# Moving group C's input projections beside group B's attention, and storing the latents of group A unsplit: a two-layer hybrid encoder on one core

## The chip, the cores and the metric

The kernel runs on one core of one Trainium2 chip. The metric is device time in microseconds of one execution of the whole program. All times below come from the profiled execution of the kernel before, or from its three timed runs.

## The reference, cut to what matters

The program computes two encoder layers over 1,024 tokens of width 1,024. A layer has four groups of attention heads side by side, one output projection, and a squared-ReLU MLP.

```
for l in range(DEPTH):                       # DEPTH = 2
    h = rms_norm(x, norm1_g[l])
    proj = h @ w_in[l]
    (a_cq, a_ckv, a_kr, b_q, b_k, b_v, c_q, c_k, c_v, d_q, d_k, d_v) = split(proj)
    y_a = mla_mixer(a_cq, a_ckv, a_kr, ...)  # A: q = rms_norm(cq) @ w_uq, k = rms_norm(ckv) @ w_uk, v = ... @ w_uv
    y_b = diff_mixer(b_q, b_k, b_v, ...)     # B: two softmaxes, p0 - lam * p1
    y_c = swa_mixer(c_q, c_k, c_v, ...)      # C: keys within +-128 tokens, with sinks
    y_d = na_mixer(d_q, d_k, d_v, ...)       # D: neighbourhood on a grid 64 wide
    mix = concat(rms_norm(y_a), y_b, rms_norm(y_c), rms_norm(y_d))
    x = x + mix @ w_out[l]
    h = rms_norm(x, norm2_g[l])
    x = x + square(relu(h @ w_up[l])) @ w_down[l]
return rms_norm(x, final_norm_g)
```

`cq` has 192 columns (128 and 64) and `ckv` has 128. These three pieces, of 128, 64 and 128 rows once transposed, are called the latents here. Every entry is float32.

## The kernel before, in words

**Numbers in two parts.** Everything is held transposed, features on partitions and tokens along the row. A matmul operand is split in two, `hi` (rounded) and `lo` (the rest), and a product takes three matmuls: w_hi x_hi, w_hi x_lo, w_lo x_hi (`passes`, lines 220 to 222). `split` (lines 190 to 199) makes the two parts: one activation on ACT (line 194, or 197 where a gain is multiplied in), and one subtraction, on DVE or POOL through the helper at line 188, or on DVE at line 198 where there is a gain.

**The stages of a layer.** The normed input `xs` is split once into 16 tiles of 128x1024, which fill the pool `big` (16 buffers) completely. Then come these stages:

- The six projections of group B run in two waves.
- Group B's attention (`attn_b`) runs with other projections between its steps. `weave` takes one step of the main work, then as many steps of the fill as the ratio allows. A step of a projection is one half: 24 matmuls of 128x512 into one PSUM tile, and its evacuation.
- Group D's attention (`attn_d`, banded: scores at line 977, transposes at 986, products at 998 and 999), with a fill of its own.
- Group C's attention, then group A's, with the first half of the output projection as fill, and then the rest of the output projection.
- The MLP, which is more than half of the time.

**What is fill for what.** Beside B stand `proj_latent` (three projections, which also make the rotary key of A) and `proj_d` (six projections). Beside D stand `proj_c` (four projections: two of queries, one of keys, one of values) and `latent_up`. `latent_up` loads the latents from DRAM, multiplies them by the up-projections (loaded as `w_lat`) into A's q, k and v, and stores those.

```
fill = chain(self.proj_latent(l, one, xs, rb, tabs, lat, krd, rows), proj_d())
self.weave(chain.from_iterable(self.attn_b(l, t, qb, kb, vb, y["b"]) for t in range(2)),
           fill, self.RB, self.LB, every=self.EV[0])
...
fill = chain(proj_c(), self.latent_up(l, lat, rows, qa, ka, va))
self.weave(self.attn_d(l, qd, kd, vd, y["d"]), fill, self.RD, self.LD, every=self.EV[1])
```

The ratios are `RB = (7, 8)`, eight steps of fill for seven of B, and `RD = (3, 2)`.

**The latents' way.** `latent_parts` squares each half of a latent for the norm (ACT, line 652; PE, line 655), splits it with its gain, and stores both parts to DRAM. `latent_up` loads them as `latp` tiles. The 64-row latent is loaded twice, into the upper and the lower half of a tile. The six `latp` tiles, and `rq` and `rkv` (the norms' rows, spread over all partitions), come from the pool `big`, so each waits until one of the 16 `xs` tiles is free, which is when the last projection that reads it is done.

**What orders the work.** The order of the steps above gives each instruction a priority. A scheduler, when the program is built, then sets one fixed order for each engine, moving ahead what it expects to be ready. An engine executes its list in order: an instruction that waits holds up all that stand behind it. Nearly all DMAs are issued from SP's queue, and one that waits there holds up the others too.

**Other lines the change touches.** `rstd_cols` (line 261) gets column sums by matmuls, and `spread` loads the rows that `rows_of` stored into all partitions. With two groups (`g=2`, only in `sub_norm` of group B) the stored rows of the groups alternate.

Of the kernel before, what the change touches and what calls it, by code (L numbers as in the profile page):

```python
# [13 lines left out]
F = mybir.dt.float32  # L14
R = mybir.dt.float32r
# [5 lines left out]
P = 128  # L21
S = 1024
# [6 lines left out]
T_CQ, T_CQR, T_CKV = 0, 1, 2  # L29
# [69 lines left out]
def layout(i):  # L99

    def padded(a, axis):

        z = np.zeros([1 if n == axis else s for n, s in enumerate(a.shape)], a.dtype)
        return np.concatenate([a, z], axis)

    n = LAYERS
    out = host_constants()
    out["x"] = i["x"][0].T.reshape(8, P, S)
    out["w_in"] = tiles_of(padded(i["w_in"], 2)[:, :, np.concatenate(input_tiles())], 4)

    wo = i["w_out"].reshape(n, 8, P, DM)[:, [2, 3, 6, 7, 4, 5, 0, 1]].reshape(n, DM, DM)
    out["w_out"] = tiles_of(wo, 4)
    out["w_up"] = tiles_of(i["w_up"], 4)
    out["w_down"] = tiles_of(i["w_down"], 4)

    uq = i["mla_w_uq"].reshape(n, 192, 4, 96)
    cols = [uq[..., 64:96].reshape(n, 192, 4, 2, 16).transpose(0, 1, 3, 2, 4).reshape(n, 192, P)]
    cols += [uq[:, :, 2 * t:2 * t + 2, 0:64].reshape(n, 192, P) for t in range(2)]
    q = np.stack(cols, 1)

    q = np.concatenate([q, q[:, :, 128:192]], 2).reshape(n, 6, P, P)
    kv = [i[w][:, None, :, t * P:(t + 1) * P] for w in ("mla_w_uk", "mla_w_uv") for t in range(2)]
    w = np.concatenate([q] + kv + [np.zeros((n, 2, P, P), uq.dtype)], 1)
    out["w_lat"] = w.reshape(n, 3, 4, P, P).transpose(0, 1, 3, 2, 4)
    rpb = padded(i["na_rpb"].reshape(n, 4, 465), 2)
    rpb[..., 465] = NEG
    out["bias"] = rpb[..., neighbours()]
    col = lambda a: a.reshape(n, -1, P).transpose(2, 0, 1).reshape(P, -1)
    gq = np.concatenate([i["mla_q_norm_g"], np.zeros((n, 64), np.float32)], 1)
    sub = np.concatenate([i["diff_subln_g"]] * 2, 1)  # L130
    lam = np.stack([i["diff_lambda_" + s] for s in ("q1", "q2", "k1", "k2")], 1)
    wide = lambda a: np.broadcast_to(a.reshape(1, -1), (P, a.size))
    out["par"] = np.concatenate(
        [col(i["norm1_g"]), col(i["norm2_g"]), i["final_norm_g"].reshape(8, P).T]
        + [col(i["out_g_" + s]) for s in ("mla", "swa", "na")]
        + [col(i["mla_kv_norm_g"]), col(gq), col(sub), wide(i["swa_sinks"])], 1)
    out["lam"] = wide(lam)
    return {k: np.ascontiguousarray(v) for k, v in out.items()}
# [7 lines left out]
class Trunk:  # L146
# [107 lines left out]
    def rstd_cols(self, sq, count, rhs, tag="mm"):  # L254

        nc = self.nc
        g = rhs.shape[1]
        n = sq.shape[1] // P
        ps = self.bank(tag, [P, n * g])
        for t in range(n):  # L260
            nc.tensor.matmul(ps[:, t * g:(t + 1) * g], sq[:, t * P:(t + 1) * P], rhs, start=True, stop=True)
        ms = self.cp.tile([P, n * g], F, tag="ms", name="ms")
        nc.vector.tensor_scalar(ms, ps, 1.0 / count, EPS, ALU.mult, ALU.add)
        return self.rsqrt_cols(ms)
# [15 lines left out]

    def spread(self, dst, rows, j=0, g=1):

        src = rows.rearrange("(t g) p -> g t p", g=g)[j]
        n = dst.shape[0]
        self.load(dst.rearrange("p (t q) -> p t q", t=8), src.partition_broadcast(n))

    def spread_here(self, dst, col):

# [88 lines left out]
    def attention(self, l):  # L377
        nc, tc, d = self.nc, self.tc, self.d
        rb = self.rb
        sbuf = lambda name, side="left": tc.tile_pool(name=f"{name}{l}", bufs=1, reuse_waits="tile", side=side)  # L380
        w_in = lambda t: d["w_in"][l, t]
        dr = lambda shape, name: self.dram.tile(shape, F, tag=name, bufs=1, name=name)
# [3 lines left out]
        qb, kb, vb = dr([2, 2, 4, 16, 2, S], "qb"), dr([2, 2, 4, 16, 2, S], "kb"), dr([4, P, 8, P], "vb")  # L386
        qd, kd, vd = dr([2, 2, P, S], "qd"), dr([2, 2, P, S], "kd"), dr([4, P, 8, P], "vd")
        qc, kc, vc = dr([2, 2, 2, 32, 2, S], "qc"), dr([2, 2, 32, 2, S], "kc"), dr([2, P, 8, P], "vc")
        lat, krd = dr([2, 3, P, S], "lat"), dr([2, 16, 2, S], "krd")
        qa = dr([2, 2, P, S], "qan"), dr([2, 4, 16, 2, S], "qar")  # L390
        ka, va = dr([2, 2, P, S], "kan"), dr([4, P, 8, P], "va")

# [25 lines left out]
        rows = []  # L418
        y = {"b": [], "d": [], "c": [], "a": []}
        with ExitStack() as stack, ExitStack() as att:  # L420
            self.ap = att.enter_context(sbuf("att"))
            with self.banks(mm=2, tr=2, sb=3, pv=1):
                with sbuf("proj", "right") as self.pp:
                    first = [w_in(t) for t in self.WAVES[0]]
                    saved = d["x"]
                    ahead = self.first
                    if l:
                        saved = self.dram.tile([8, P, S], F, tag="saved", bufs=1, name="saved")
                        for k in range(8):
# [12 lines left out]
                    tabs = self.table("32", rb, nc.vector)  # L442
                    self.eng = nc.vector
                    for t in range(2):
                        for ev, b in zip(evacs_b(t), banks):
                            raw = self.ptile()
                            for n in range(2):
                                sl = slice(n * 512, n * 512 + 512)
                                nc.scalar.activation(raw[:, sl], b[n], AF.Copy)
                                ev(n, raw[:, sl])  # L450
                        if t == 0:
                            banks = wave()
                            self.several([w_in(t) for t in self.WAVES[1]], xs, banks)
                        self.eng = nc.gpsimd

                    fill = chain(self.proj_latent(l, one, xs, rb, tabs, lat, krd, rows), proj_d())
                    self.weave(chain.from_iterable(self.attn_b(l, t, qb, kb, vb, y["b"]) for t in range(2)),
                               fill, self.RB, self.LB, every=self.EV[0])
                    self.tails.append(self.mix_b(mix, y["b"], self.gsub[:, l:l + 1]))
                    fill = chain(proj_c(), self.latent_up(l, lat, rows, qa, ka, va))  # L460
                    self.weave(self.attn_d(l, qd, kd, vd, y["d"]), fill, self.RD, self.LD, every=self.EV[1])
                gout = lambda n: self.gout[n][:, l]
                self.tails.append(self.mix_group(mix, 2, y["d"], gout("na")))
# [72 lines left out]
    EV = (.5, .5, .7, 1)  # L536
    EARLY, RC, RA, LA = 4, (8, 1), (3, 1), 0
    WAVES = [(T_BQ[t], T_BK[t], T_BV[t]) for t in range(2)]
    NP, RB, RD, LB, LD = 6, (7, 8), (3, 2), 40, 50

    def weave(self, main, fill=iter(()), ratio=(1, 0), lead=0, end=True, every=1):

# [101 lines left out]
            self.keep(dst[:, :, n * 4:n * 4 + 4].rearrange("h p k e -> p h (k e)"), b.bitcast(F))  # L644
        return then

    def latent_parts(self, y, g, rows, n, dst, squares):

        nc = self.nc
        sl = slice(n * 512, n * 512 + 512)  # L650
        sq = self.part()
        nc.scalar.activation(sq[:rows], y[:rows], AF.Square)
        ps = self.bank("mm", [P, 4])
        for t in range(4):
            nc.tensor.matmul(ps[:, t:t + 1], sq[:rows, t * P:(t + 1) * P], self.ones[:rows, 0:1],
                             start=True, stop=True)
        nc.vector.tensor_copy(squares[:, n * 4:n * 4 + 4], ps)
        self.emit_parts(y[:rows], [(dst[:, :rows, sl].rearrange("a p s -> p a s"), slice(0, rows))],
                        slice(0, rows), g[:rows])

    def proj_latent(self, l, one, xs, rb, tabs, lat, krd, rows_out):


        nc = self.nc
        squares = [self.col("sq%d" % i, 8) for i in range(3)]
        for i, t, g in ((0, T_CQ, self.gq[:, l, 0:1]), (2, T_CKV, self.gkv[:, l:l + 1])):
            yield from one(t, xs, self.ev_plain(rb, lambda n, y: self.latent_parts(y, g, P, n, lat[:, i], squares[i])))
        c, s = tabs

        def ev(n, ps):  # L670
# [8 lines left out]
            self.emit_parts(y[64:112], [  # L679
                (krd[:, :, h, sl].rearrange("a p s -> p a s"), slice(64 + 32 * h, 80 + 32 * h))  # L680
                for h in range(2)], slice(64, 112))
            self.latent_parts(y, self.gq[:, l, 1:2], 64, n, lat[:, 1], squares[1])

        yield from one(T_CQR, xs, ev)
        q, k = squares[0], squares[2]
# [6 lines left out]
    def latent_up(self, l, lat, rows, qa, ka, va):  # L692
# [2 lines left out]
        self.spread(rq, rows[0])  # L695
        self.spread(rkv, rows[1])
        parts = []
        for i, r in ((0, P), (1, 64), (2, P)):
            p = []
            for j in range(2):  # L700
                t = self.big_tile(R, "latp")
                for at in range(0, P, r):
                    self.load(t.bitcast(F)[at:at + r], lat[j, i, :r])
                p.append(t)
            parts.append(tuple(p))
        tabs = self.table("32", rq, nc.gpsimd)
        (qn, qr), kn = qa, ka

# [782 lines left out]
```

## Time and profile before

| What | us |
|---|---|
| Three timed runs | 2729.50, 2731.64, 2728.26 (median 2729.5) |
| The profiled execution | 2728.97 |
| Its span, first to last instruction | 2727.2 |
| PE busy | 2553.1 (94%) |
| DVE busy | 1994.1 (73%) |
| ACT busy | 1430.9 (52%) |
| POOL busy | 1134.5 (42%) |

The mean granted clock of TensorE is 0.967. Matmuls overlap in a pipeline, so that a matmul of 128x512 is shown as some 390 ns long while the next one starts 0.23 us after it; "PE busy" therefore hides small gaps. Times in the views are microseconds from the first instruction, and the first layer's attention lies between 0 and about 700 us, the second one's between about 1372 and 2050 us.

### The profile page before, as it was taken

Reading aid. Unit: us, or ns where it says so; the run is one execution under the profiler, and the core shown is the slowest. Engines: PE = TensorE matmul, PEld = TensorE weight load, DVE = VectorE, ACT = ScalarE, POOL = GpSimd, SP = SyncE. Lnnn points to the kernel's source line nnn. Section 1 sums busy time; section 2 is a strip of 40 time slices with the busy share of each in tenths; the row PEclk is TensorE's granted clock in tenths of the full one; section 3 lists DMA queues with packets and bytes.
Section 4 is the critical chain, followed back from the end, with each engine's and each line's share of the span. In section 5 each row is a group of like instructions: output and inputs, shape, how many; then the busy total and the mean of one; then the engine's idle time right before and its main releaser. Section 6 shows DMA issues by size and latency. Waiting matters only on the chain.

```text
span 2727.2 us, 37613 instructions
## 1 busy us (share of the span) xinstructions
PE 2553.1 (94%) x12298; PEld 2110.1 (77%) x12298; DVE 1994.1 (73%) x3544; ACT 1430.9 (52%) x2547; POOL 1134.5 (42%) x754
## 2 busy tenths in 40 slices
PE   8989988899989999999999899889998999999997
PEld 6778876787778887888877688767886788878886
DVE  7787767674966669787567778677749666687786
ACT  4667757563534444444436676576635344444444
POOL 2555642111245554445435556331013455545552
PEclk9989999999989999999998899899999999999998
DMA  5534597231234447444244345972221444664431
GB/s 175 166 105 126 154 280 241 83 93 40 65 130 156 151 160 267 156 138 142 98 133 138 95 134 157 300 215 71 76 70 44 154 159 149 223 222 150 131 100 62
DMA packets 190516, 389.20 MB, mean 143 GB/s; under 512 B 23712, under 2 KB 30832, under 8 KB 190320
## 3 DMA queue, kind: packets, MB, share of 16 engines
q1 hardware_dynamic: 176496, 361.62, 43.0%
q10 hardware_dynamic: 13824, 25.17, 2.7%
q8 instruction: 98, 1.61, 0.3%
q14 instruction: 98, 0.80, 0.1%
HBM read 263.29 MB, written 123.41 MB: 142 GB/s over the span
## 4 chain that ended last, share of the span: by engine, by line
PE 70%; DVE 14%; DMA 7%; ACT 4%; issue 3%; SPq 1%; POOL 1%; DVEq 0%; ACTq 0%; POOLq 0%
PE u L220 8%; PE u L222 8%; PE u L221 8%; PE mm L220 5%; PE mm L221 5%; PE mm L222 5%; PE p L220 5%; PE p L221 5%; PE p L222 5%; PE sb L804 3%; PE tr L840 2%; DVE p L806 2%; DVE part L188 2%; PE pv L829 2%; PE pv L828 2%
## 5 line engine op out<-in xcount | busy, mean ns | idle before, releaser
L188 POOL TENSOR_TENSOR wl<-raw,wh 128x512 fp32r<-128x512 f32 x448 | 635.1, 1418 | 705.2 <-ACT wh L194 690.1
L194 ACT ACTIVATE wh<-raw 128x512 fp32r<-128x512 f32 x448 | 281.5, 629 | 579.8 <-PE u L221 315.0
L188 POOL TENSOR_TENSOR wl<-ws,wh 128x512 fp32r<-128x512 f32 (+1 forms) x112 | 148.1, 1325 | 456.9 <-ACT wh L194 426.0
L220 PE MATMUL u<-far,wh 128*128 128x512 f32 x768 | 301.5, 393 | 11.5 <-ACT ev L1237 8.3
L188 DVE TENSOR_TENSOR raw<-raw 128x512 f32<-128x512 f32 x256 | 226.4, 890 | 107.4 <-POOL wl L188 56.9
L222 PE MATMUL u<-far,wl 128*128 128x512 f32 x768 | 300.5, 391 | 1.9 <-POOL wl L188 1.9
L221 PE MATMUL u<-far,wh 128*128 128x512 f32 x768 | 300.3, 391 | 0.0
L188 DVE TENSOR_TENSOR ptl<-tr,pth 128x512 fp32r<-128x512 f32 (+2 forms) x384 | 238.3, 628 | 66.6 <-ACT pth L194 64.9
L809 ACT ACTIVATE p<-p,nm 128x1024 f32<-128x1024 f32 x192 | 220.1, 1147 | 99.8 <-DVE nm L806 98.9
L194 ACT ACTIVATE pth<-tr 128x512 fp32r<-128x512 f32 (+2 forms) x384 | 205.6, 546 | 121.0 <-PE tr L840 64.8
L220 PE MATMUL p<-far,wh 128*128 128x512 f32 x640 | 251.7, 393 | 7.6 <-DVE ev L188 7.6
L222 PE MATMUL p<-far,wl 128*128 128x512 f32 x640 | 250.9, 392 | 1.5 <-POOL wl L188 1.5
L221 PE MATMUL p<-far,wh 128*128 128x512 f32 x640 | 251.0, 392 | 0.0
L804 PE MATMUL sb<-stack 96*128 96x512 f32 x640 | 218.5, 424 | 24.7 <-DVE nm L806 24.0
L188 DVE TENSOR_TENSOR far<-act,far 128x512 fp32r<-128x512 f32 x224 | 208.6, 960 | 14.6 <-ACT far L194 14.6
L188 POOL TENSOR_TENSOR p<-p 128x1024 f32<-128x1024 f32 x64 | 154.3, 2415 | 141.1 <-ACT p L893 125.0
L220 PEld LDWEIGHTS u<-far,wh 128*128 128x128 f32 x768 | 145.4, 189 | 43.6 <-ACT ev L1237 9.2
L222 PEld LDWEIGHTS u<-far,wl 128*128 128x128 f32 x768 | 145.0, 189 | 33.2 <-POOL wl L188 2.7
L220 PE MATMUL mm<-xh,wh 128*128 128x512 f32 x416 | 169.4, 407 | 0.8 <-DVE rows L272 0.2
L806 DVE CUSTOM_DVE_ANT_0 p<-sb,zero,nm 128x512 f32<-128x512 f32 x192 | 142.4, 743 | 36.3 <-PE sb L804 32.8
L221 PEld LDWEIGHTS u<-far,wh 128*128 128x128 f32 x768 | 145.3, 189 | 30.2
L221 PE MATMUL mm<-xl,wh 128*128 128x512 f32 x416 | 166.6, 400 | 0.0
(243 smaller groups left out, 6147.0 us busy)
## 6 DMA issues: line engine op xcount, KB each, us to landing
act<-acts SPq DMA_DIRECT2D x224, 256.0 KB
raw<-in_w_up SPq DMA_DIRECT2D x128, 256.0 KB
acts<-ev SPq DMA_DIRECT2D x128, 256.0 KB
raw<-in_w_down SPq DMA_DIRECT2D x128, 256.0 KB
acts<-ev ACTq DMA_DIRECT2D x96, 256.0 KB
ws<-in_w_in SPq DMA_DIRECT2D x76, 256.0 KB
rz<-drows SPq DMA_DIRECT2D x40, 256.0 KB
stack<-kd SPq DMA_DIRECT2D x32, 256.0 KB
```

The lines of the kernel that those rows point to most:

```text
L188: (eng or self.nc.vector).tensor_tensor(out=out, in0=a, in1=b, op=op)
L194: nc.scalar.activation(hi, src, AF.Copy)
L220: mm(ps, w[0], x[0][:, sl], start=start, stop=False)
L221: mm(ps, w[0], x[1][:, sl], start=False, stop=False)
L222: mm(ps, w[1], x[0][:, sl], start=False, stop=stop)
L804: self.nc.tensor.matmul(ps, q[:, qt * P:(qt + 1) * P], k[:, sl], start=i == 0, stop=i == len(passes) - 1)
L806: self.nc.vector.tensor_tensor_reduce(out=p[:, sl], in0=ps, in1=self.zero[:, 0:1].bitcast(F).broadcast_to([P, 512]), scale=-scale, scalar= ...
L809: self.nc.scalar.activation(p, p, AF.Exp, bias=nm[:, 1:2], scale=-1.0, accum_out=z)
L828: nc.tensor.matmul(out, v[:, kt], h[:, sl], start=kt == 0, stop=False)
L829: nc.tensor.matmul(out, v[:, kt], lo[:, sl], start=False, stop=kt == 7)
L840: nc.tensor.transpose(t[:, k * 256 + i * P:k * 256 + (i + 1) * P], p[:, (j * 2 + k) * P:(j * 2 + k + 1) * P], self.ident)
```

## The change

Four edits, all in the attention part:

- `proj_c` becomes the last part of B's fill, and the ratio `RB` becomes `(2, 3)`, three steps of fill for two of B. The 18 steps of B then take 27 steps of fill: 7 of `proj_latent`, 12 of `proj_d`, 8 of `proj_c`. D's fill is `latent_up` alone.
- The latents are stored unsplit, as one part (`latent`), straight from the tile that the evacuation wrote.
- `latent_up` loads each latent once (the 64-row one into both halves of a tile, as before) and splits it there, with the gain: six splits of 128x512. The gain of the 64-row latent is now laid out for both halves.
- For two groups, the columns in `rstd_cols` are ordered by group, so that `spread` reads one contiguous run of 4 KB for each partition where it read eight runs of 512 bytes.

```diff
-    gq = np.concatenate([i["mla_q_norm_g"], np.zeros((n, 64), np.float32)], 1)
+    gq = np.concatenate([i["mla_q_norm_g"], i["mla_q_norm_g"][:, 128:192]], 1)
...
-            nc.tensor.matmul(ps[:, t * g:(t + 1) * g], sq[:, t * P:(t + 1) * P], rhs, start=True, stop=True)
+            nc.tensor.matmul(ps.rearrange("p (g t) -> p t g", g=g)[:, t], sq[:, t * P:(t + 1) * P], rhs,
+                             start=True, stop=True)
...
-        src = rows.rearrange("(t g) p -> g t p", g=g)[j]
-        n = dst.shape[0]
-        self.load(dst.rearrange("p (t q) -> p t q", t=8), src.partition_broadcast(n))
+        src = rows.rearrange("(g t) p -> g (t p)", g=g)[j]
+        self.load(dst, src.partition_broadcast(dst.shape[0]))
...
-        lat, krd = dr([2, 3, P, S], "lat"), dr([2, 16, 2, S], "krd")
+        lat, krd = dr([3, P, S], "lat"), dr([2, 16, 2, S], "krd")
...
-                    fill = chain(self.proj_latent(l, one, xs, rb, tabs, lat, krd, rows), proj_d())
+                    fill = chain(self.proj_latent(l, one, xs, rb, tabs, lat, krd, rows), proj_d(), proj_c())
...
-                    fill = chain(proj_c(), self.latent_up(l, lat, rows, qa, ka, va))
+                    fill = self.latent_up(l, lat, rows, qa, ka, va)
...
-    NP, RB, RD, LB, LD = 6, (7, 8), (3, 2), 40, 50
+    NP, RB, RD, LB, LD = 6, (2, 3), (3, 2), 40, 50
...
-    def latent_parts(self, y, g, rows, n, dst, squares):
+    def latent(self, y, rows, n, dst, squares):
...
+        self.keep(dst[:rows, n * 512:n * 512 + 512], y[:rows])
         sq = self.part()
         nc.scalar.activation(sq[:rows], y[:rows], AF.Square)
...
-        self.emit_parts(y[:rows], [(dst[:, :rows, sl].rearrange("a p s -> p a s"), slice(0, rows))],
-                        slice(0, rows), g[:rows])
...
-        for i, r in ((0, P), (1, 64), (2, P)):
-            p = []
-            for j in range(2):
-                t = self.big_tile(R, "latp")
-                for at in range(0, P, r):
-                    self.load(t.bitcast(F)[at:at + r], lat[j, i, :r])
-                p.append(t)
-            parts.append(tuple(p))
+        for i, (r, g) in enumerate(((P, self.gq[:, l, 0:1]), (64, self.gq[:, l, 1:2]), (P, self.gkv[:, l:l + 1]))):
+            t = self.big_tile(F, "latent")
+            for at in range(0, P, r):
+                self.load(t[at:at + r], lat[i, :r])
+            h, lo = self.big_tile(R, "lath"), self.big_tile(R, "latl")
+            for sl in self.halves():
+                self.split(h[:, sl], lo[:, sl], t[:, sl], g)
+            parts.append((h, lo))
```

More of the change, by code (lines that the diff above doesn't have):

```diff
@@ L645, in to_values @@
         return then
-    def latent_parts(self, y, g, rows, n, dst, squares):
+    def latent(self, y, rows, n, dst, squares):
         nc = self.nc
-        sl = slice(n * 512, n * 512 + 512)
+        self.keep(dst[:rows, n * 512:n * 512 + 512], y[:rows])
         sq = self.part()
@@ L665, in proj_latent @@
         squares = [self.col("sq%d" % i, 8) for i in range(3)]
-        for i, t, g in ((0, T_CQ, self.gq[:, l, 0:1]), (2, T_CKV, self.gkv[:, l:l + 1])):
-            yield from one(t, xs, self.ev_plain(rb, lambda n, y: self.latent_parts(y, g, P, n, lat[:, i], squares[i])))
+        for i, t in ((0, T_CQ), (2, T_CKV)):
+            yield from one(t, xs, self.ev_plain(rb, lambda n, y: self.latent(y, P, n, lat[i], squares[i])))
         c, s = tabs
@@ L681, in ev @@
                 for h in range(2)], slice(64, 112))
-            self.latent_parts(y, self.gq[:, l, 1:2], 64, n, lat[:, 1], squares[1])
+            self.latent(y, 64, n, lat[1], squares[1])
         yield from one(T_CQR, xs, ev)
```

## The prediction

> **What bounds the kernel now.** I read the page first, then a table by stage (the windows view), then the chain of waits of the stage that stands out, then the waits of TensorE in it. The page says that TensorE (PE) is busy nearly throughout.
>
> ```profile
> span 2727.2 us, 37613 instructions
> PE 2553.1 (94%) x12298; PEld 2110.1 (77%) x12298; DVE 1994.1 (73%) x3544; ACT 1430.9 (52%) x2547; POOL 1134.5 (42%) x754
> ```
>
> The change touches only the attention of each layer, so the share of the whole says little. The table by stage shows the end of group B's attention (300 to 343 us), the last projections (343 to 365), group D (365 to 424) and group C (424 to 470), and below them the second layer's last projections, D and C. The columns are busy microseconds of each engine with its instructions, then the granted clock, the DMA engines' busy share, and GB/s.
>
> ```profile
> core 0: us, PE busy (x) PEld busy (x) DVE busy (x) ACT busy (x) POOL busy (x), PEclk, DMA share, GB/s
> 300.00:343.00 43.00, 42.90 (x236) 36.84 (x236) 32.83 (x79) 30.39 (x53) 35.00 (x22) 1.00 0.59 154
> 343.00:365.00 22.00, 21.77 (x123) 18.53 (x122) 12.20 (x32) 11.83 (x29) 5.85 (x5) 1.00 1.00 296
> 365.00:424.00 59.00, 44.67 (x240) 36.65 (x238) 40.00 (x103) 34.08 (x84) 22.06 (x15) 0.91 0.99 286
> 424.00:470.00 46.00, 38.34 (x204) 29.38 (x204) 37.19 (x104) 35.85 (x97) 12.36 (x8) 0.96 0.75 240
> 1690.00:1712.00 22.00, 21.77 (x124) 18.89 (x123) 13.03 (x39) 14.68 (x38) 10.07 (x7) 1.00 0.98 282
> 1712.00:1770.00 58.00, 46.55 (x243) 39.86 (x242) 38.24 (x99) 32.16 (x80) 23.30 (x15) 0.85 1.00 295
> 1770.00:1820.00 50.00, 41.98 (x219) 33.72 (x219) 37.08 (x107) 34.72 (x90) 12.37 (x8) 0.90 0.85 253
> ```
>
> Up to 343 us PE has no gap and the DMA engines are 59% busy. From 343 to 424 they are full, and from 365 on PE is idle for 14.3 of 59 us at a clock of 0.91. The second layer repeats this. So B is PE's stage and D is the DMA engines' stage. The chain of waits, in order of time (start, length, what), says the same:
>
> ```profile
> 358.15 7.51 DMA rkv<-drows
> 365.69 11.75 DMA latp<-lat
> 399.02 5.40 DMA bias<-in_bias
> 404.43 9.07 DMA stack<-kc
> 413.57 9.20 DMA kan<-both
> ...
> 1713.22 10.30 DMA latp<-lat
> 1723.60 11.52 DMA stack<-kd
> ```
>
> The loads of the latents stand on it in both layers. What PE itself waits for in the first layer's D (total, times, longest):
>
> ```profile
> PE mm L720 <- DMA latp<-lat: 2.7, 2, 2.2
> PE mm L221 <- DMA latp<-lat: 2.4, 1, 2.4
> PE mm L220 <- DMA latp<-lat: 1.3, 1, 1.3
> ```
>
> That is 6.4 us of idle PE in a layer, and it is the part of D that the change can reach most directly.
>
> **The projections of C.** They are 4 tiles of 48 matmuls, 192 in a layer. Their spacing, and that of B's products and transposes, is read from the chain, where one step is the time to the next start:
>
> ```profile
> 352.59 0.44 PE tr L840 x4
> 353.03 0.12 PE pv L828
> 353.95 0.23 PE mm L220
> ```
>
> So 192 x 0.23 = 44 us a layer. It looks as if 44 us of PE moved out of a stage with gaps into one without, which would be a loss. It isn't: in the order of PE's instructions before, only 5 projection matmuls stand behind the last one of B, because the scheduler had already pulled C's projections ahead beside B. After the change none do. On PE the move is worth 5 x 0.23 = 1.2 us, which I count as nothing. The POOL work of C's projections (35.00 of 43 us in B's end) is likewise beside B in both, only spread over more steps; I cost it at nothing, with B's PE work as its cover. If that cover were gone, a step of B would wait for POOL's instructions, of 1.3 to 2.4 us each.
>
> What does move is the place of the latents' products. Before, all of B's matmuls stand ahead of the first product of a latent. After, 56 of them (24 transposes, 32 products) stand behind it, and 26 of the 54 latent products stand ahead of B's last matmul. So the `xs` tiles are free, and rq, rkv, the tables and the latents are loaded, while B still has 24 x 0.11 + 32 x 0.12 = 6.5 us of PE work left. The full stretch of DMA begins that much earlier beside PE's work: worth from 0 to 6.5 us a layer. I take half, 3.3, since loads and stacks of D queue at the same place, and SP's list is in order.
>
> **The bytes.** The latents' loads of both layers are these:
>
> ```profile
> latp<-lat SPq DMA_DIRECT2D x8, 512.0 KB
> ...
> latp<-lat SPq DMA_DIRECT2D x8, 256.0 KB
> ```
>
> A layer loads 4 x 512 + 4 x 256 KB = 3.15 MB; half goes, 1.57 MB. At 286 to 296 GB/s that is 5.4 us of DMA time, in a stretch where DMA ends last, and the latp step of the chain (11.75 and 10.30 us) has room for it. The stores halve as well, but beside B, where the DMA share is 0.59: nothing. They now go straight from the tile that holds the evacuated half; there are three such tiles, and one is held until its store has landed. Six stores a layer; the nearest row, a store of B's keys, took this long:
>
> ```profile
> 63.64 4.37 DMA kb<-both
> ```
>
> Against a projection half of 24 x 0.23 = 5.5 us that is covered; if it isn't, the evacuation behind it waits on DVE and PE for its bank, at most some 4 us a layer. I take 0. The contiguous spread touches two loads of 256 KB per call, two calls a layer, one of them in the full stretch: at most 0.9 us (half of 0.52 MB at 290 GB/s), taken as 0.
>
> **The splits.** Six of 128x512 leave B's projections (two of them with half the partitions, which saves no time) and six come to `latent_up`, each one ACT and one DVE instruction. The same forms before:
>
> ```profile
> L198 DVE SCALAR_TENSOR_TENSOR both<-part,par,both 128x512 fp32r<-128x512 f32 x8 | 8.7, 1092 | 1.2 <-ACT both L197 1.2
> L198 DVE SCALAR_TENSOR_TENSOR opl<-x,par,oph 128x512 fp32r<-128x512 f32 x16 | 11.7, 744 | 2.0 <-ACT oph L197 2.0
> L197 ACT ACTIVATE oph<-x,par 128x512 fp32r<-128x512 f32 x16 | 11.5, 716 | 16.1 <-DVE x L188 16.1
> ```
>
> On ACT 6 x 0.72 = 4.3 us, on DVE between 6 x 0.74 = 4.5 and 6 x 1.09 = 6.6. As work they fit: in D's 59 us DVE is idle for 19 and ACT for 25. As latency the first counts: 0.72 + 1.09 = 1.8 us between the latent's landing and its first product. The other two latents can be split while PE does the first one's products. I count 1.8 us a layer, between 0 and 5.4 (all three). What leaves B is worth 0, as PE's list there is full, and at most 6.6 us, if DVE were what B waits for; the row that could say so is this one, for 60 to 343 us:
>
> ```profile
> PE sb L804 <- DVE nm L806: 10.9, 7, 5.0
> ```
>
> Half of it is a single wait in the norms of the latents, which the change keeps, so I stay at 0.
>
> Why the same form takes 744 or 1092 ns shows nearby. These are two DVE instructions on 8 columns, and the POOL instructions beside the first:
>
> ```profile
> 163.87 1.92 DVE L688 TENSOR_SCALAR sq<-sq 128x8 f32<-128x8 f32 x1
> 171.66 0.28 DVE L251 SCALAR_TENSOR_TENSOR rs_r<-rs_t,rs_r 128x8 f32<-128x8 f32 x2
> ...
> L188 POOL TENSOR_TENSOR tabc<-tabc,rb x2: 2354/2366/2377, 163.4 to 1510.1; 128x1024 f32<-128x1024 f32 x2
> ```
>
> The slow one begins at 163.87 while POOL runs from 163.4, and ends at 165.8, when POOL does. The Trainium skill ("SBUF — State Buffer", section "SBUF: two separate sides") states that DVE and GpSimd share one pair of ports under an exclusive lock, so that the loser waits for the whole instruction; the trace agrees, with 1.92 us against 0.14. By that rule one split that meets POOL could be held by a whole POOL instruction. In D POOL is busy for 22.06 of 59 us, so the mean of 1.09 us is nearer than 0.74, and I keep it.
>
> **The sum.** For each layer -5.4 (bytes) - 3.3 (earlier start) + 1.8 (split) = -6.9 us, for two -13.8. The profiled execution took 2728.97 us, 1.8 more than its span; that less 14 gives 2715 us. It stands 0.5 us under the median of the three runs, which I don't correct.
>
> **Rivals.** *All of it is won.* If the earlier start is worth its full 6.5 us, and PE no longer waits for latents (6.4 us here; I use it for both layers), each layer gives 5.4 + 6.5 + 6.4 = 18.3 us, and the time is 2729 - 37 = 2692. For it speaks that the chain runs through these loads twice; against it that the waits behind them (bias, stack, kan) are DMA too and stay, and that the loads still begin only when `xs` is free.
>
> *Slower: PE's list is held up earlier.* In the new order only 15 matmuls stand between the last projection and the first latent product, and behind that product wait the 56 matmuls of B and D's first scores. Before, this is how long the way from rq's issue to the first product was:
>
> ```profile
> 357.72 0.33 SPq L160 DMA_DIRECT2D rq<-drows  x1
> ...
> 366.98 0.50 PE L220 MATMUL mm<-latp,wh 128*128 128x512 f32 x1 [1.33 <-DMA latp<-lat]
> ```
>
> That is 9.3 us, with the split 11.1. The cover is the rest of the last projection after two pairs of `xs` are free (18 x 0.23 = 4.1 us) and some 30 small matmuls of B and D in and behind it (about 4.4 us): 8.5 us. My forecast has a stall of 2.6 us there, in place of 1.3. The rival has all three splits on the path (5.4 us) and the six DVE instructions ahead of B's last score minima, each at 1.09 (6.5 us), less 5.4 for the bytes: 6.5 us a layer, 2729 + 13 = 2742. It decides once the way from `xs` to a split latent is longer than about 12 us, that is, when D's stack loads go first while the DMA engines are full.
>
> *Nothing.* D's heads wait for stacks, whose slots come free only as heads finish. If those set the pace, the bytes saved are bytes nobody waits for, and the time stays at 2729.
>
> **How the numbers follow.** The forecast (2715, between 2700 and 2723) gets 0.42, all of it 0.17, nothing 0.13, slower 0.28. A change of 0.2%, 5.5 us, is about what the runs can tell from none. That makes 0.59 for faster, 0.13 for the same, 0.28 for slower. The range reaches from 2690, just under the first rival, to 2743, just over the slower one; beyond them lie the unknown ends (three splits held by POOL, held store tiles), with under 2 in 10.
>
> **What would show it.** Right: the DMA share is near 1 from before B's end; the latent step of the chain falls from 11.75 and 10.30 us to 5 or 6; in the window from B's end to C's end PE's idle time falls by some 5 us; six DVE splits of about 1 us appear there. Wrong: PE waits for `lath` or `latl` by more than 6.4 us a layer, with B's transposes behind it; or C starts when it did, with the same waits for stack and bias; or B grows by more than D shrinks, which would say that C's projections were not free there.

## The result and the profile after

The changed kernel takes 2760.97 us (median of four runs, 2756.58 to 2765.87), the kernel before 2728.88 (four runs, 2725.40 to 2731.64). The ratio is 1.0109, with a 95% interval of 1.0092 to 1.0125: slower by 32 us, outside the predicted range and on its wrong side.

The page of the changed kernel, span and busy times:

```profile
span 2757.4 us, 37594 instructions
PE 2563.6 (93%) x12298; PEld 2116.2 (77%) x12298; DVE 2001.2 (73%) x3544; ACT 1435.2 (52%) x2547; POOL 1140.8 (41%) x754
```

The table by stage over the first four stretches of the prediction's table (busy us of each engine, granted clock, DMA share, GB/s):

```profile
300.00:343.00 43.00, 40.59 (x227) 34.16 (x227) 38.14 (x83) 27.06 (x46) 26.00 (x17) 1.00 0.41 111
343.00:365.00 22.00, 13.93 (x67) 11.48 (x65) 13.93 (x29) 14.38 (x25) 12.72 (x6) 0.79 0.79 225
365.00:424.00 59.00, 48.81 (x257) 41.53 (x256) 45.94 (x109) 35.86 (x89) 20.25 (x13) 0.85 0.93 258
424.00:470.00 46.00, 30.53 (x141) 24.27 (x141) 28.68 (x78) 27.02 (x68) 11.04 (x7) 0.80 0.83 259
```

Before, PE was busy for 42.90, 21.77, 44.67 and 38.34 us in them. Two stretches got worse: 343 to 365, where B's last softmaxes now stand, by 7.8 us, and 424 to 470, where D passes into C, by 7.8 us, while in 365 to 424 PE is busy for 4.1 us more. The granted clock in these three is lower too, 0.79 to 0.85 where it was 0.91 to 1.00, and B's products of 128x256 between 330 and 400 us are shown 327 and 341 ns long on average where they were 304 and 287. The first layer's MLP begins its products at 737.7 us instead of 721.5: 16 us for one layer, half of the loss. The MLPs themselves take as long as before, within 1 us (634 and 641 us from the first to the last product before; the two are a little under half of the time), so the loss lies in the attention of both layers.

The steps that the prediction spoke of can be read in three views of the changed kernel: its chain of waits, the waits of PE between 340 and 425 us, and the splits of the latents (duration least, median, most, in ns).

```profile
350.46 9.41 DMA latent<-lat
368.56 2.81 DVE latl L198
377.07 3.85 DVE latl L198 x2
```

```profile
PE mm L638 <- DVE part L188: 6.6, 1, 6.6
PE mm L718 <- DVE latl L198: 1.8, 1, 1.8
```

```profile
L198 DVE SCALAR_TENSOR_TENSOR latl<-latent,par,lath x6: 750/2054/2894, 355.9 to 379.2; 128x512 fp32r<-128x512 f32 x6
```

The load of the latent is still on the chain with 9.41 us, not 5 or 6, and the splits are slower than I took them. But PE waits for them for 1.8 us only. The larger hole is elsewhere. This is VectorE's list after 438 us, where D's scores are done:

```profile
438.66 0.20 DVE L755 RECIPROCAL rz<-z 128x8 f32<-128x8 f32 x1
442.81 0.28 DVE L273 COPY rows<-mm 8x128 f32<-8x128 f32 x1 [3.95 <-DMA drows<-rows]
443.02 1.39 DVE L198 SCALAR_TENSOR_TENSOR mixl<-rz,g_sub,mixh 128x512 fp32r<-128x512 f32 x2
444.34 0.27 DVE L273 COPY rows<-mm 8x128 f32<-8x128 f32 x1
446.95 0.48 DVE L1082 CUSTOM_DVE_ANT_0 p<-sb,mask,nsink 128x256 f32<-128x256 f32 x1 [2.34 <-DMA mask<-in_swa]
...
449.73 0.68 DVE L188 TENSOR_TENSOR y<-pv,pvt 64x512 f32<-64x512 f32 x1 [1.75 <-DMA yb<-y]
```

and PE's in the same place:

```profile
439.29 0.27 PE L271 MATMUL mm<-ident,rz 128*8 128x128 f32 x1
447.50 1.65 PE L975 MATMUL sb<-stack 128*128 128x384 f32 x4 [7.93 <-DVE nb L1082]
450.47 0.79 PE L1025 MATMUL pv<-zero 128*128 128x512 f32 x1 [1.32 <-DVE y L188]
```

The rows and mixl instructions are steps of B's and D's tails: what follows a head once its last product is done (reciprocal of the denominators, rows to DRAM and back over all partitions, for B a second norm, the store `yb`, its load and the split for the output projection). VectorE waits for three DMAs one behind the other, with C's first softmax and D's output queued behind them: for two stores of the tails (`rows` and `yb`), and between them for the load of C's mask, which is no part of a tail and goes out at 440.4 us, when D's last scores are done. PE has nothing to do for 7.9 us. Before, its waits for C's softmax between 425 and 462 us came to 3.3 us, and the longest was 2.3:

```profile
PE sb L977 <- DVE nb L1084: 3.3, 3, 2.3
```

The last row of VectorE's shows a tie between B and D. Group B's output and D's come from `ypair`, which has two buffers; D's second pair of heads writes into the buffer in which B's second output sits until B's tail has stored it. That store (line 167), before and after:

```profile
L167 SPq DMA_DIRECT2D yb<-y x1: 337/337/337, 406.2 to 406.2; - x1
```

```profile
L167 SPq DMA_DIRECT2D yb<-y x1: 527/527/527, 444.0 to 444.0; - x1
  DVE y L188: 1.8, 1
```

Before, no engine waited for it. After, it is issued 38 us later, and D's output waits 1.8 us for it at the end of VectorE's waits. B's last output, on which its tail works, is written 29.5 us later too, before and after:

```profile
362.58 0.69 DVE L188 TENSOR_TENSOR y<-pv,pvt 64x512 f32<-64x512 f32 x1 [3.67 <-ACT pvt L746]
```

```profile
392.06 0.68 DVE L188 TENSOR_TENSOR y<-pv,pvt 64x512 f32<-64x512 f32 x1
```

### The profile page after: what moved, and what is told of

It reads as the page before. It is cut to its first block, busy times and chain, and to the rows that moved or that the text cites. A ratio compares the mean times of both kernels' runs of the same rounds, so it can differ in the third digit from the quotient of the medians.

```text
span 2757.4 us, 37594 instructions
## 1 busy us (share of the span) xinstructions
PE 2563.6 (93%) x12298; PEld 2116.2 (77%) x12298; DVE 2001.2 (73%) x3544; ACT 1435.2 (52%) x2547; POOL 1140.8 (41%) x754
## 4 chain that ended last, share of the span: by engine, by line
PE 72%; DVE 14%; DMA 5%; ACT 4%; issue 3%; POOL 1%; SPq 0%; DVEq 0%; ACTq 0%; POOLq 0%
PE u L220 8%; PE u L222 8%; PE u L221 8%; PE mm L220 5%; PE mm L221 5%; PE mm L222 5%; PE p L220 5%; PE p L221 5%; PE p L222 5%; PE sb L802 3%; DVE p L804 2%; PE tr L838 2%; DVE part L188 2%; PE pv L827 1%; PE pv L826 1%
## 5 line engine op out<-in xcount | busy, mean ns | idle before, releaser
L188 POOL TENSOR_TENSOR wl<-raw,wh 128x512 fp32r<-128x512 f32 x448 | 641.9, 1434 | 695.6 <-ACT wh L194 660.2
```

The source lines that it names most:

```text
L188: (eng or self.nc.vector).tensor_tensor(out=out, in0=a, in1=b, op=op)
```

## Experiments

**The change in parts.** The first four kernels take the change apart.

*The move alone*, with the latents and the spread as before:

```diff
-fill = chain(self.proj_latent(l, one, xs, rb, tabs, lat, krd, rows), proj_d())
+fill = chain(self.proj_latent(l, one, xs, rb, tabs, lat, krd, rows), proj_d(), proj_c())
...
-fill = chain(proj_c(), self.latent_up(l, lat, rows, qa, ka, va))
+fill = self.latent_up(l, lat, rows, qa, ka, va)
...
-NP, RB, RD, LB, LD = 6, (7, 8), (3, 2), 40, 50
+NP, RB, RD, LB, LD = 6, (2, 3), (3, 2), 40, 50
```

> The kernel before with only C's projections moved into B's fill and the ratio (2, 3); latents still stored in two parts, spread as before. Theory 1 (the loss is the splitting of the latents, whose ACT and DVE instructions wait for a load ahead of the end of B): nothing to split, so the earlier place of the latents' products costs little: 2720 to 2735 us. Theory 2 (the loss is the move: B's stage is full and its engines' lists get longer): most of the 32 us is here, 2748 to 2762 us.

Measured: 2763.7 us, ratio 1.0124 (1.0107 to 1.0141). The move alone is the whole loss, 1.7 us more than the range of the second theory.

*The latents alone*: the changed kernel with these three edits and the spread undone.

> The kernel before with only the latents stored unsplit and split after loading; projections, ratio and spread as before. Theory 1a (the six splits cost by themselves, wherever they stand): 2745 to 2762 us. Theory 1b (they cost because the move puts them ahead of the end of B): here B is over before the first latent product, so 2723 to 2735 us. Theory 2: 2720 to 2730 us, by the bytes saved rather below than above.

Measured: 2725.5 us, ratio 0.9984 (0.9974 to 0.9993). This part is a gain of 4 us.

*The spread alone*: only the edits in `rstd_cols` and `spread`.

> The kernel before with only the contiguous spread of the two-group rows. All theories: no change that can be told, 2725 to 2732 us; a change above that would say that a small edit shifts the scheduler's whole order by as much.

Measured: 2732.5 us, ratio 1.0004 (0.9992 to 1.0016): nothing, as predicted.

*The changed kernel with the ratio as it was.*

```diff
-NP, RB, RD, LB, LD = 6, (2, 3), (3, 2), 40, 50
+NP, RB, RD, LB, LD = 6, (7, 8), (3, 2), 40, 50
```

> The changed kernel with the ratio back at (7, 8): of the 27 steps of fill 20 go between B's steps, the other seven (C's) behind them. Theory 1b (splits ahead of B's end): the xs tiles are free later against B, so few splits stand ahead of B's end, and most of the loss goes: 2728 to 2740 us. Theory 1a: it stays, 2745 to 2762 us. Theory 2 (the density of the fill in B): most goes, as in theory 1b, and the move alone is as slow as the whole change.

Measured: 2748.5 us, ratio 1.0069 (1.0054 to 1.0084): most of the loss stays, against theories 1b and 2, and 1a has fallen with the latents alone. B's last softmax (its last reciprocal, line 888) is back at 332.5 us (363.2 after, 336.9 before), and still over half of the loss is there. So it isn't a late end of B by itself. The windows of 425 to 450 us show where PE runs dry, first before and after:

```profile
425.00:450.00 25.00, 19.80 (x108) 15.69 (x107) 21.14 (x60) 19.98 (x56) 7.60 (x6) 0.97 0.74 246
```

```profile
425.00:450.00 25.00, 13.98 (x66) 10.80 (x66) 13.63 (x42) 13.77 (x35) 8.20 (x6) 0.83 0.84 270
```

and then in the move alone, in this kernel, and in the latents alone:

```profile
425.00:450.00 25.00, 10.87 (x49) 8.14 (x49) 9.71 (x28) 8.44 (x19) 8.64 (x6) 0.70 0.93 279
```

```profile
425.00:450.00 25.00, 9.63 (x36) 7.10 (x36) 10.36 (x27) 7.79 (x16) 9.25 (x7) 0.62 0.82 265
```

```profile
425.00:450.00 25.00, 19.48 (x94) 14.49 (x93) 17.50 (x49) 18.43 (x47) 8.71 (x6) 0.86 0.82 269
```

One window is no measure of the whole loss: this kernel's is emptier than the changed kernel's, and it loses less.

**The tails earlier.** This led to the theory of the tails. In the program the tails, B's and D's own, are written between D's steps, one piece every second step (`EV[1]`, .5). The next run writes one at every step, and changes nothing else in the changed kernel.

```diff
-EV = (.5, .5, .7, 1)
+EV = (.5, 1, .7, 1)
```

> The changed kernel with one number of EV changed (.5 to 1 for D's stage), so that B's tails are written into the program at every step of D and not at every second one. In the static order of VectorE's list this brings the splits of B's last output (mixl from rz) from behind C's 16th softmax instruction, and the rows of B's second norm from D's 56th to its 44th; projections and the order of the latents' products stay. Theory crowding: the move loses because B's tails, a chain of DMA round trips, now come due where C starts, VectorE's and ScalarE's lists stand behind them and TensorE has no projection left to do there (425 to 450 us: TensorE busy 13.98 of 25 after, 19.80 before). Then half of the loss or more goes: 2738 to 2750 us, and 425 to 450 gets back to 18 or more of 25. Theory late end: it is the end of B, 26 us later, behind which D has the same length whatever the tails do. Then 2756 to 2766 us and D's last softmax stays at about 437 us.

Measured: 2729.4 us, ratio 1.0001 (0.9989 to 1.0013). All of the loss is gone for one number: 31.5 us by the medians, 29.5 by the two ratios, and more than was expected. The same window, and the store of B's second output, in this run:

```profile
425.00:450.00 25.00, 19.41 (x110) 15.41 (x109) 19.84 (x55) 19.38 (x52) 9.31 (x6) 0.97 1.01 297
```

```profile
L167 SPq DMA_DIRECT2D yb<-y x1: 319/319/319, 421.4 to 421.4; - x1
```

B's last softmax is at 362.6 us as after, and its last output is written at 386.7, still 24 us later than before. So B's late end stayed and the loss went: the theory of the late end falls.

*The same, and the latents' products spread over all of D* (`RD` from (3, 2) to (5, 2)).

> As the run before, and RD from (3, 2) to (5, 2), so that the latents' products are spread over the whole of D and up to C's start, as they were before the change (VectorE's list has four of their evictions beside C's first 12 softmax instructions). Theory crowding with missing cover: 2732 to 2746 us, a few us under the run before, the stretch 425 to 450 at 19 or more of 25. Theory late end: 2756 to 2768 us.

Measured: 2736.6 us, ratio 1.0024 (1.0007 to 1.0040), 7 us over the run before, not under it, though the two intervals overlap. PE is busy for 22.16 of 25 us in the window, as expected, and the time is no better for it. So what the earlier tails gave is not bettered by more cover for PE at C's start.

*The kernel before with the tails earlier.*

> The kernel before with that same number of EV changed: the control for the two. Theory crowding: little to gain, since the tails did not crowd there; 2722 to 2734 us. If the earlier tails are good by themselves, whatever was moved, it gains as much here as in the changed kernel: 2710 to 2720 us. It also holds the projections back to D's 48th softmax instruction and the latents' products to C's 44th in VectorE's list, which may cost: up to 2745 us.

Measured: 2744.3 us, ratio 1.0052 (1.0032 to 1.0071). There the same number costs 13 us, so earlier tails aren't good in themselves. B's store goes out at 381.1 us, and the last product of a projection starts at 381.7 instead of 363.4. But that isn't where the time goes: the first layer's MLP begins at 719.6 us, 2 us earlier than before, and the loss is all in the second layer, whose MLP begins 728.6 us after the last product of the first layer's MLP instead of 711.5. What makes it there stays open.

*The move alone with the tails earlier.*

> The move alone (the first of the runs, 2763.7 us) with EV's number for D's stage at 1. Theory crowding: the loss goes here too, whatever the form of the latents: 2728 to 2742 us. If the recovery needs the latents split behind the load: 2750 us or more.

Measured: 2731.2 us, ratio 1.0009 (0.9997 to 1.0021): 32 us come back here too, whatever the form of the latents.

**The loss without the move.** The kernel before with the tails written less often:

```diff
-EV = (.5, .5, .7, 1)
+EV = (.5, .35, .7, 1)
```

> The kernel before, nothing moved, with EV's number for D's stage from .5 to .35: B's tails are written into the program less often. In VectorE's static list the rows of B's second norm and the splits of its last output then stand behind C's 4th to 8th softmax instruction, as in the run with the old ratio, while B's end, the projections and the head of the latents' products stay as they were. Theory crowding: the loss of the move appears without the move: 2740 to 2760 us, with TensorE under 15 of 25 in 425 to 450 us. If the tails were only a help that the move happened to need, and their place is not the loss itself: 2726 to 2736 us.

Measured: 2741.8 us, ratio 1.0047 (1.0032 to 1.0061). Nothing is moved, and 12.5 us are lost, at the low end of what was expected and 38% of what the move costs; PE has 17.39 of 25 us in the window, more than the 15 expected. B's store goes out at 434.6 us.

```profile
L167 SPq DMA_DIRECT2D yb<-y x1: 319/319/319, 434.6 to 434.6; - x1
```

*Half of the move*: C's queries beside B, its keys and values again ahead of `latent_up`, `RB` (7, 9).

```diff
+def proj_ckv():
+    yield from one(T_CK, xs, self.ev_rope(ct, kc))
+    yield from one(T_CV, xs, self.ev_plain(rb, self.to_values(vc)))
...
+fill = chain(proj_ckv(), self.latent_up(l, lat, rows, qa, ka, va))
```

> The changed kernel with half of C's projections moved: its queries beside B, its keys and values again at the head of D's fill (RB (7, 9)). VectorE's list has the rows of B's second norm at D's 54th softmax instruction and the last splits at C's 12th, between before and after. Theory crowding: between the two, 2728 to 2745 us. If what is moved costs in itself, half of the loss: 2738 to 2744 us; if only the last of the fill matters, no loss: 2720 to 2728 us.

Measured: 2728.7 us, ratio 0.9999 (0.9987 to 1.0011), at the low edge of what crowding gives, and within 0.7 us of the range for "only the last of the fill matters", so the two can't be told apart here. That the loss goes with the amount moved does not hold. The store goes out at 414.8 us.

**What in the tail holds.** Three runs take single waits away and leave the place of the tail. First, B's second output is split straight from its tile, without the store and the load:

```diff
+            direct[0][1] = self.mixed(y, direct[1])
...
-        kept = self.dram.tile([P, S], F, tag="yb", bufs=2, name="yb")
-        self.keep(kept, y)
```

> The changed kernel, EV as it was, but B's second pair of heads is not stored and loaded again: it is split straight from its tile at the end of its norm, so that one store and one load (3.3 to 7 us each there) and the waits on them leave the tail; the place of the rows of B's second norm stays at D's 56th softmax instruction. Theory crowding, with the DMA trips as what holds the lists at C's start: a third to two thirds of the 31 us come back, 2740 to 2752 us, and TensorE's 7.9 us wait at 439 us gets shorter by half or more. If the trips are not what holds the lists but only the number of instructions there: 2753 to 2764 us.

Measured: 2756.2 us, ratio 1.0087 (1.0069 to 1.0105). Only some 5 or 6 us of 32 come back, if any (the interval overlaps that of the changed kernel), and the time lies in the range of the second theory, not of the first. So the store and the load are not what holds most of it. The buffer is now free when the splits have read it, and D's output follows them, at 443.90 us instead of 449.73:

```profile
440.30 0.28 DVE L273 COPY rows<-mm 8x128 f32<-8x128 f32 x1 [3.67 <-DMA drows<-rows]
441.71 0.28 DVE L273 COPY rows<-mm 8x128 f32<-8x128 f32 x1 [1.14 <-DMA drows<-rows]
441.92 1.39 DVE L198 SCALAR_TENSOR_TENSOR mixl<-y,g_sub,mixh 128x512 fp32r<-128x512 f32 x2
...
443.90 0.67 DVE L188 TENSOR_TENSOR y<-pv,pvt 64x512 f32<-64x512 f32 x1
```

PE's wait did not go. It now waits for that output instead (line 1029 prepares the PSUM bank `pv`, of which there is one, for D's next half; the view is of 425 to 462 us):

```profile
PE pv L1029 <- DVE y L188: 7.9, 3, 7.4
```

VectorE still stands in copies into the tile `rows`, of which there are two, each free again when its store has landed. So the other two runs give it a third buffer, in the changed kernel and in the move alone:

```diff
-sb = self.cp.tile([n, P], F, tag="rows", name="rows")
+sb = self.cp.tile([n, P], F, tag="rows", bufs=3, name="rows")
...
-dr = self.dram.tile([n, P], F, tag="rows", bufs=4, name="drows")
+dr = self.dram.tile([n, P], F, tag="rows", bufs=8, name="drows")
```

> The changed kernel with one more buffer for the tile rows (3, 2 before) and eight in DRAM (4 before): every copy of a row into that tile waits until the store of the copy two places ahead has landed, now three places ahead. The order of all instructions stays. At C's start five such copies stand close together, and VectorE stands in them for 3.9 us in the first layer and 2.3 us in the second (drows<-rows). If those stores are what holds the list: 2748 to 2756 us. If the next late DMA of the crowd (mask, rz<-yb, rz<-drows) takes their place: 2757 to 2765 us.

> The move alone (2763.7 us, where VectorE stands in these copies for 7.2 us of the first and 11.7 us of the second layer, the most of all) with the third buffer, the order of all instructions as in the move alone. If those stores are what holds the list: 2742 to 2754 us. If the next late DMA takes their place: 2755 to 2766 us.

Measured: 2759.3 us, ratio 1.0113 (1.0088 to 1.0139), and 2761.8 us, ratio 1.0132 (1.0103 to 1.0161): nothing in either, as the second theory has it. What VectorE waits for longest between 424 and 462 us in the first of them:

```profile
DVE mixl L198 <- ACT mixh L197: 4.4, 1, 4.4
DVE y L188 <- DMA yb<-y: 4.3, 1, 4.3
```

The wait for `rows` is gone, and the next trip of the same chain ends last. So neither of these two waits is the cause by itself. That the chain as a whole is late is the reading that is left; no run takes away all of its waits with the tail in its place.

**All but the move**, and what is left:

> The changed kernel with the move alone undone (fills of B and D and RB as before): the latents unsplit in DRAM and the new spread together. If the parts add up: e2 gave -4.2 and e3 +1.0 of a bound of 3, so 2722 to 2729 us, faster than both kernels. If the contiguous rows shorten the round trips behind D's start, some us less: 2715 to 2722 us.

Measured: 2722.6 us, ratio 0.9973 (0.9963 to 0.9982). Without the move the change is a gain of some 7 us, at the edge between the two ranges.

*The same with the tails a little earlier* (`EV[1]` .6).

> The changed kernel with the move undone (2722.6 us) and EV's number for D's stage from .5 to .6. If the tails still stand a little late there, 2714 to 2722 us; since the kernel before lost 13 us at 1 because its projections were held back, rather the same or worse: 2720 to 2732 us.

Measured: 2725.1 us, ratio 0.9987 (0.9975 to 0.9999): no better.

*The same with a third buffer for `rows`.*

> The changed kernel with the move undone (2722.6 us) and the same third buffer, as a candidate that beats both kernels by more. These waits are 0.8 us there: 2719 to 2726 us by either theory.

Measured: 2719.5 us, ratio 0.9966 (0.9950 to 0.9982), the fastest kernel of the case. It beats both; over the run without the third buffer the intervals overlap.

Last, the 7 us between the changed kernel with early tails (2729.4) and all but the move (2722.6). The tables of the latents go from GpSimd to VectorE, in each of the two:

```diff
-tabs = self.table("32", rq, nc.gpsimd)
+tabs = self.table("32", rq, nc.vector)
```

> The run with the tails at every step (2729.4 us) with the two products of the latents' rotary tables on VectorE in place of GpSimd. What is left of the loss: that run is 7 us over the one with all but the move (2722.6). Its TensorE has 17.0 of 25 busy us in 350 to 375 us, where the latents' splits run beside GpSimd's tables (2.4 us each) and take 1.9 to 3.9 us in place of 0.74. If the splits beside GpSimd are that rest: 2721 to 2727 us, with every split under 1.3 us. If it is the loads, which wait for the same DMA engines: 2727 to 2733 us.

> The changed kernel with the move undone (2722.6 us) and the same two products on VectorE. If the splits beside GpSimd hold the latents there too, 2716 to 2721 us; if not, 2720 to 2728 us.

Measured: 2737.6 us, ratio 1.0018 (1.0007 to 1.0029), and 2723.5 us, ratio 0.9972 (0.9957 to 0.9987). In the first the splits did get shorter:

```profile
L198 DVE SCALAR_TENSOR_TENSOR latl<-latent,par,lath x6: 734/747/1168, 358.4 to 376.6; 128x512 fp32r<-128x512 f32 x6
```

a median of 747 ns in place of 950, and a most of 1.17 us in place of 2.88, and yet the time is no better: 8 us slower by the medians, 5 by the ratios, whose intervals overlap. (The longest split of the run with GpSimd's tables took 2.88 us, not the 3.9 of the expectation.) VectorE now has the tables' two products to do, 1.23 and 1.22 us, so the run is not the shorter splits alone. It gives no sign that the splits are where these 7 us are; where they are stays open.

**The runs side by side.** For each kernel, in the one execution that was traced: when B's second output is stored, and when the first output of D's second pair is written, in the first and in the second layer.

| Kernel | stored at, us | first output at, us | ratio |
|---|---|---|---|
| all but the move, third `rows` | 411.6, 1754.7 | 419.2, 1762.8 | 0.9966 |
| all but the move | 417.0, 1764.2 | 424.7, 1773.9 | 0.9973 |
| before | 406.2, 1759.3 | 417.7, 1772.0 | 1 |
| after, half of the move | 414.8, 1773.2 | 422.9, 1777.0 | 0.9999 |
| after, early tails | 421.4, 1763.7 | 436.2, 1785.7 | 1.0001 |
| after, early tails, tables on VectorE | 418.9, 1771.9 | 444.3, 1789.8 | 1.0018 |
| before, late tails | 434.6, 1785.8 | 437.3, 1789.7 | 1.0047 |
| before, early tails | 381.1, 1739.8 | 409.8, 1768.7 | 1.0052 |
| after, old ratio | 437.6, 1792.4 | 441.2, 1795.9 | 1.0069 |
| after, no trip | none (split) | 443.9, 1807.2 | 1.0087 |
| after | 444.0, 1800.9 | 449.7, 1809.0 | 1.0109 |
| after, third `rows` | 440.5, 1807.7 | 446.3, 1815.5 | 1.0113 |
| the move alone | 443.5, 1807.1 | 447.3, 1810.9 | 1.0124 |
| the move alone, third `rows` | 453.5, 1821.8 | 457.3, 1825.3 | 1.0132 |

The six kernels not listed lie between 0.9972 and 1.0024, with first outputs at 417 to 435 us. From "before, late tails" down the output follows the store by 3 to 8 us, the length of the trip and of what stands ahead in the list, and the later it is, the slower the kernel, in the main. In the rows above it mostly follows by 8 to 25 us and waits for something else. "Before, early tails" fits neither: its outputs are the earliest in the first layer, and it loses 13 us all the same.

What is shown is that the place of the tails in D's stage makes the loss: one number takes the whole of it away, in the changed kernel and in the move alone, and brings 12.5 us of it where nothing is moved. The number moves B's tail and D's own together. That the loss acts through B's tail, the shared buffer and the lists behind it is read from these times and waits, and the run without the trip says that the store by itself is a small part; a third buffer for `y`, which would show the part of the buffer directly, was not tried.

## Why the prediction was wrong, point by point

- **"B is PE's stage and D is the DMA engines' stage"** held in the main (DMA share 0.93 in 365 to 424 us after, where B's last products now stand too), but I didn't ask which work ties the two. B's tail runs in D's stage, and I never put it on the list of what the move shifts.
- **The move, "which I count as nothing"**, is the step that failed. It measured +33 us by itself, +38 on top of the other edits (2761.0 against 2722.6). My argument, that only 5 projection matmuls stood behind B's last one, is about PE's work, whose amount indeed didn't change (12298 matmuls in both). The count was right: in the trace 5 stand behind it before and none after. What changed is the order. C's projections now stand ahead of B's end, whose last softmax moves from 336.9 to 363.2 us and whose last output from 362.6 to 392.1, while D's fill has eight steps less. B's tail, whose store came 44 us after that output before and comes 52 us after it now (at 406.2 and 444.0), ran beside projections and D before, and now comes out where D's second pair needs its buffer and C starts. The runs show that the loss goes when the tails are written earlier.
- **The earlier place of the latents' products, -3.3 us a layer.** They did begin 5 us earlier in the first layer (362.1 for 367.0), and 5 us later in the second (1723.9 for 1719.1). The matmuls of B behind the first latent product, which I counted as 6.5 us of PE's work and read as a gain, were the sign of B's later end: the last of them starts at 390.8 us, 28.7 us behind that product.
- **The bytes, -5.4, and the splits, +1.8 us a layer.** The latents alone measured -4.3 us for both layers (0.16% of 2729) where these two terms give -7.2: right in sign, and some 60% in size (the interval reaches from -2 to -7). The splits were mis-sized: in the changed kernel a median of 2.05 us and up to 2.89 in the first layer, not 0.74 to 1.09. The rule on the ports that the prediction cites from the Trainium skill ("SBUF — State Buffer", section "SBUF: two separate sides") fits that. In the kernel with early tails the most in the first layer is 1.17 us with the tables off GpSimd, and 2.88 with them. It bears on the splits, not on the loss.
- **The spread at nothing** was right: it measured +0.04%, with zero inside its interval. The stores at nothing were not measured apart; they are a part of the latents alone.
- **The slower rival, "PE's list is held up earlier"** (2742, 0.28), had the sign and a part of the place: PE does wait 6.6 us on line 638 at B's end. But its price hung on the split latents, and the move alone, with latents stored in two parts, is the slowest of the first four runs. With early tails a wait of 4.5 us on line 638 is still there and the loss is gone; the wait of 7.9 us that goes with the loss ends at 447.5 us, 89 us behind the one on line 638, where neither the forecast nor a rival looked. The sign for it that I named, "B grows by more than D shrinks", came true: B's last output comes 29.5 us later, and from there to D's last output it takes 81.3 us where it took 80.0. As I had written, that says that C's projections were not free beside B; the runs add that the price lies in the tails that wait for B's end.

## What to carry to other kernels

When work is moved ahead of a stage's end, count not only its own engine time but the chain that hangs on that end: when it comes out now, which buffer it releases and who needs that buffer. Where filler is taken from a stage, move the due times of the side work in that stage with it: one such number was worth some 30 us here, as much as the whole loss, and the same number cost 13 us in the kernel before. A change of several edits is best priced edit by edit; here a gain of some 7 us stood behind a loss of 38.

## What the runs showed that I had not expected

- A split of 128x512 on VectorE, 0.75 us where nothing stands beside it, took up to 2.89 us beside GpSimd. In the changed kernel one starts at 368.48 us, 0.02 us after a GpSimd instruction, and ends at 371.37, 0.5 us after it:

```profile
368.46 2.37 POOL L188 TENSOR_TENSOR p<-p 128x1024 f32<-128x1024 f32 x1 [6.80 <-ACT p L891]
368.48 2.89 DVE L198 SCALAR_TENSOR_TENSOR latl<-latent,par,lath 128x512 fp32r<-128x512 f32 x1
```

- The granted clock was lower in stretches in which PE stood still: 0.62 in 425 to 450 us with PE busy for 9.63 of 25 (the changed kernel with the old ratio), 0.97 in the same stretch with 19.41 (early tails). It isn't a fixed relation: the run with `RD` (5, 2) has 22.16 us there and 0.84. What the lower clock itself cost was not measured apart.
